# LoRA products on halves of the rows, head sums on quarters of the columns, one partition range for both inverses, and a corrected ordering clock

## The chip, the cores and the metric

One core of a Trainium2 chip. The time is that of the device, from the first to the last instruction of the program, in microseconds (us); several runs are made and their median is compared. The core's engines each work through their own queue, in order: TensorE (PE, with its weight loads shown apart as PEld), VectorE (DVE), ScalarE (ACT), GpSimd (POOL) and SyncE (SP), which here only issues DMAs. PE writes to PSUM, eight banks of 512 float32 in each of 128 partitions. ACT and DVE read the banks.

## The reference

One inference step of a one-layer decoder on 1024 new prompt tokens and 32 sample tokens (8 sequences of 4), with 1024 channels: an RWKV-7 branch and an RG-LRU branch on the same input, gated and merged, an output projection, a layer norm, a SwiGLU feed-forward part and a second layer norm. What matters here is the RWKV-7 branch:

```
w = -softplus(-(w0 + tanh(w_lo) @ w2)) - 0.5        # w_lo: 64 columns of the mixed input
decay = exp(-exp(w))
a = sigmoid(a0 + a_lo @ a2)                         # a_lo: 64 columns
kk = k * k_k;  kk = kk / max(sqrt(sum over the head of kk*kk), 1e-12)
k = k * (1 + (a - 1) * k_a)
per token and head (64 x 64 state S):
    sa = S @ (-kk)
    S  = S * w + outer(sa, kk * a) + outer(v, k)
    y  = S @ r
```

The kernel computes the recurrence in chunks of 64 tokens: inside a chunk a 64 x 64 triangular system per head is inverted (by blocks of 16 and 32), and a state is carried from chunk to chunk. All products that carry weights are done with numbers split in a rounded part (fp32r) and a remainder: three matmuls for one product.

## The kernel before

The tokens are worked in two passes of 512 (in the first with the 32 sample tokens and 8 rows of shift in front, 548 columns in use, in the second 512), the channels in four pairs of 128-channel tiles. A pass and a pair make a **unit** (u, 0 to 7); a unit has two tiles (i), four heads, and for the inverses two halves (g) of four chunks each.

Two kinds of work share PE. The main stream (`gemm_tile`, line of the profile L246 for its matmuls) goes through the input projection tile by tile, 24 wide matmuls for each piece, into two banks in turn; ACT and DVE empty them. Everything else is background: `load2` and `wkv_tile` (LoRA products, decays, rates, head sums), `stage` (copies into the layout of the chunks), `inverse`, `chain` (the recurrence over the eight chunks), `finish`, `lru`, `sample`. Background matmuls use three banks in common (`Bk`) and three of the chain's own. Since a helper records nearly every operation, most instructions have the line L316 in the profile and are told apart by the names of their tiles.

The order on each engine is written out when the kernel is built. Background work is written as generators; between the main stream's matmuls `tick` issues the waiting operations that can start soonest by a **clock** (`Clock`), a table of costs per operation with a time per engine. Where `gemm_tile` or `until` finds nothing free, the clock is advanced. On the chip the engines then run that order, and semaphores make them wait where the clock was wrong.

The places that the change touches:

- `load2(lora, ...)` brings the two LoRA matrices of a unit into `lora`, [128, 2, 2, 128]: w2 (64 rows) on partitions 0 to 63 and a2 on 64 to 127, each in a block of its own with zeros on the other partitions. `wa` holds tanh(w_lo) on partitions 0 to 63 and a_lo on 64 to 127.
- `wkv_tile` multiplies the first block, and then the second, with all 128 rows of `wa` (`bg_mm`, three matmuls a piece; pieces of 292 and 256 columns in the first pass and one of 512 in the second), and ACT takes tanh out of the bank into `t1` and `t4`.
- The head sums: `t6` holds the squares of k; a float32 matmul with `sel` ([128, 128], two columns in use) sums each head's 64 channels. Two rows of the bank go back into `t6` and by four DMAs to a scratch in DRAM (`ssd`), from where `wkv` loads them into `n2` in the layout of the inverses.
- `inverse(u, g)`: a chain of 30 short DVE operations on 64 partitions (`bn`, `bt`, `btmp`), 0 to 63 for g = 0 and 64 to 127 for g = 1; then products with `n2` into `bte` and `bze`, stores to DRAM, loads back (`tdv`, `zt`), and small matmuls on 32 x 32 parts of the array.
- `chain(u)`: for each of eight chunks `cx` (matmuls), a copy of it to `xs`; `cu`, a copy of it to `su`; `cs_`, and four state updates on DVE, (i, h) for a 64-partition half h of tile i:

```
A(xs[0:64, :, 0], cx[0:64])
TC(xs[64:128, :, 1], cx[64:128])
...
A(su[0:64, :, 1, 0], cu[0:64])
TC(su[64:128, :, 1, 1], cu[64:128])
...
for i in range(2):
    for h in range(2):
        STT(to, su[hb, i, 0, h], pc[hb, i, c:c + 1], cs_[hb, i], OP.mult, OP.add)
```

`A` is an ACT activation, `TC` a DVE copy, `STT` a DVE operation of two inputs and a scalar, `MM` a matmul.

Of the kernel before, what the change touches and what calls it, by code (L numbers as in the profile page):

```python
# [9 lines left out]
F32 = mybir.dt.float32  # L10
# [27 lines left out]
C_ID, C_MP, C_SCAN, C_MS, C_MX, C_MB, C_SEL, C_BONES, C_M16, C_N = 0, 128, 256, 768, 832, 896, 904, 1032, 1160, 1161  # L38
# [38 lines left out]
class Clock:  # L77
# [6 lines left out]
    def __init__(self):  # L84
        self.t = dict.fromkeys(("PE", "ACT", "DVE", "POOL", "SP", "DMA"), 0.0)
        self.uses = {}
        self.masks = {}
        self.table = 0
        self.tile = None
        self.port = {"DVE": [], "POOL": []}  # L90
# [86 lines left out]
    def op(self, e, f, args, kw, at, last):  # L177
# [168 lines left out]
def tile_hybrid_step(ctx: ExitStack, tc: tile.TileContext, I, O):  # L346
# [131 lines left out]
    with ExitStack() as zctx:  # L478
# [69 lines left out]
        lora = [T(f"lora{i}", [128, 2, 2, 128], F32R) for i in range(2)]  # L548
# [13 lines left out]
        bn, bt, btmp = T("bn", [128, 16, 16]), T("bt", [128, 16, 16]), T("btmp", [128, 64])  # L562
        bte, bze = T("bte", [128, 16, 32]), T("bze", [128, 16, 32])
        n2s = [T(f"n2_{i}", [128, 16]) for i in range(2)]
# [25 lines left out]
        sel = cst[:, C_SEL:C_SEL + 128]  # L590
# [10 lines left out]
        for x in lora:  # L601
            pool.memset(x.bitcast(F32), 0.0)
# [89 lines left out]
        def load2(dst, src, flag, after):  # L692
# [5 lines left out]
            if len(dst[0].shape) == 3:  # L698
                split2([x.rearrange("p i m -> p (i m)") for x in dst], t[:, 0:256])
            else:  # L700
                for n in range(2):
                    b = slice(64 * n, 64 * n + 64)
                    split2([x[b, n].rearrange("p i m -> p (i m)") for x in dst], t[b, 0:256])
# [4 lines left out]
        def bg_mm(p, ops, use):  # L708

            for t0, t1 in pieces(p):  # L710
# [5 lines left out]
                Bk.put(ps)  # L716
            yield
# [10 lines left out]
        def wkv_tile(u, i, parts, side):  # L728
# [68 lines left out]
        def wkv(u):  # L797
# [14 lines left out]
            for g in range(2):  # L812
                for x in range(2):
                    sp.dma_start(n2[64 * g + 32 * x:64 * g + 32 * x + 32],
                                 ssd[g, :, :, :, 16 * x:16 * x + 16])
# [44 lines left out]
        def inverse(u, g, n2):  # L860
# [3 lines left out]
            pt = slice(64 * g, 64 * g + 64)  # L864
# [34 lines left out]
            for x in range(2):  # L899
                d = slice(16 * x, 16 * x + 16)  # L900
                sp.dma_start(bn[64 * g + 32 * x:64 * g + 32 * x + 32],
# [4 lines left out]
            pool.memset(bt[pt], 0.0)  # L906
            pool.memset(bt[pt].rearrange("p t j -> p (t j)")[:, 0:256:17], 1.0)
# [5 lines left out]
            TT(bn[pt], bn[pt], n2[pt, None, :].to_broadcast([64, 16, 16]), OP.mult)  # L913
            for s in range(15):
                m = 15 - s
                tmp = btmp[pt, 0:m * (s + 1)].rearrange("p (t j) -> p t j", j=s + 1)
                TT(tmp, bn[pt, s, s + 1:16].rearrange("p (t o) -> p t o", o=1).to_broadcast([64, m, s + 1]),
                   bt[pt, s:s + 1, 0:s + 1].to_broadcast([64, m, s + 1]), OP.mult)
                TT(bt[pt, s + 1:16, 0:s + 1], bt[pt, s + 1:16, 0:s + 1], tmp, OP.add)
            for x in range(2):  # L920
                b, d = slice(64 * g + 32 * x, 64 * g + 32 * x + 32), slice(16 * x, 16 * x + 16)
# [4 lines left out]
            for x in range(2):  # L926
                b, d = slice(64 * g + 32 * x, 64 * g + 32 * x + 32), slice(16 * x, 16 * x + 16)
# [59 lines left out]
        def chain(u):  # L987
# [68 lines left out]
            for c in range(8):  # L1056
# [8 lines left out]
                A(xs[0:64, :, 0], cx[0:64])  # L1065
                TC(xs[64:128, :, 1], cx[64:128])
# [10 lines left out]
                A(su[0:64, :, 1, 0], cu[0:64])  # L1077
                TC(su[64:128, :, 1, 1], cu[64:128])
# [11 lines left out]
                for i in range(2):  # L1090
                    for h in range(2):
# [869 lines left out]
```

## Time and profile before

| | |
|---|---|
| median of 3 runs | 2140.77 us (2139.39 to 2144.16) |
| profiled execution, its own time | 2158.58 us |
| its span, first to last instruction | 2156.8 us |
| mean granted clock of PE | 0.962 |
| matmuls, all instructions | 17664, 44027 |
| DMA | 152.85 MB, mean 71 GB/s |

The branches, which hold all that is changed, run to about 1290 us of the span; from 1400 to 2100 us PE does the feed-forward part without a pause.

In a row of the groups stand line, engine, operation, the tiles as out<-in, for PE the rows and columns of the array in use (64*128 is half of the rows), the shape, the count; then busy time, mean length of one, and idle time before. In the timeline stand start and length in us. PE's lengths overlap: how long a matmul holds the array is read from its start to the next one's. float32 matmuls are two instructions each, transposes and the rounded products one.

### The profile page before, as it was taken

The page shows a single profiled execution, that of the slowest core. Times are in us where ns is not written, and L with a number is a line of the kernel's source. Part 1 is how long each engine was busy: PE and PEld are TensorE (multiplying, and loading weights), DVE is VectorE, ACT ScalarE, POOL GpSimd, SP SyncE. Part 2 cuts the span into 40 slices and gives each one's busy share as a digit, 9 for nine tenths or more (in the row PEclk, how much of TensorE's full clock was granted, in tenths as well). Part 3 has the DMA queues.
Part 4 walks back from the last instruction along what each step waited for, and adds up shares of the span by engine and source line. Part 5 has one row for each costly group of instructions (what it writes and reads, how often), then busy time and mean ns, then how long its engine had stood idle before and what let it go on. Part 6 is the DMA issues. An engine that isn't in the chain of part 4 may idle for free.

```text
span 2156.8 us, 44027 instructions
## 1 busy us (share of the span) xinstructions
PE 2065.4 (96%) x17664; PEld 1792.2 (83%) x17664; DVE 1226.6 (57%) x2967; ACT 1070.5 (50%) x2475; POOL 389.2 (18%) x797
## 2 busy tenths in 40 slices
PE   7799999999999999999999899999999999999997
PEld 7788898897986777777777697889999999999987
DVE  5676695796877887777867666522322322222226
ACT  4656756757666677767576735821121122112221
POOL 1101210220310310211212020221211211111124
PEclk9897997999999999999999799999999999999999
DMA  4131231131241231232313323221111211111112
GB/s 137 56 92 36 66 95 48 51 107 51 76 131 60 78 97 52 67 86 67 98 58 90 113 96 133 88 69 38 61 40 35 64 40 47 37 54 49 40 50 81
DMA packets 124925, 152.85 MB, mean 71 GB/s; under 512 B 82784, under 2 KB 87296, under 8 KB 124720
## 3 DMA queue, kind: packets, MB, share of 16 engines
q0 software_dynamic: 31936, 112.75, 15.6%
q1 hardware_dynamic: 92784, 37.28, 7.0%
q8 instruction: 139, 2.28, 0.4%
q14 instruction: 66, 0.54, 0.1%
HBM read 132.45 MB, written 17.57 MB: 70 GB/s over the span
## 4 chain that ended last, share of the span: by engine, by line
PE 76%; DVE 10%; ACT 9%; issue 3%; DMA 1%; POOL 0%; SPq 0%; DVEq 0%; ACTq 0%; POOLq 0%
PE bank L246 60%; PE bank L316 15%; DVE tmp L316 2%; DVE wl L316 1%; ACT tmp L316 1%; ACT wh L316 1%; DVE su L316 1%; ACT L316 1%; ACT arm L316 1%; ACT nz L316 1%; ACT bk L316 1%; DVE btmp L316 1%; DVE bt L316 1%; DVE arm L316 1%; DVE rge L316 1%
## 5 line engine op out<-in xcount | busy, mean ns | idle before, releaser
L246 PE MATMUL bank<-xx,wh 128*128 128x512 f32 (+4 forms) x3168 | 808.3, 342 | 26.9 <-ACT xx L246 8.5
L246 PEld LDWEIGHTS bank<-xx,wh 128*128 128x128 f32 x3168 | 553.5, 196 | 88.7 <-ACT xx L246 8.5
L246 PE MATMUL bank<-xx,wl 128*128 128x512 f32 (+4 forms) x1584 | 541.3, 342 | 0.0
L316 DVE TENSOR_TENSOR wl<-wraw,wh 128x512 fp32r<-128x512 f32 (+2 forms) x336 | 264.3, 788 | 264.2 <-ACT wh L316 262.1
L316 ACT ACTIVATE wh<-wraw 128x512 fp32r<-128x512 f32 (+2 forms) x408 | 246.1, 610 | 274.6 <-PE bank L246 245.6
L246 PE MATMUL bank<-hl,wh 128*128 128x272 f32 (+1 forms) x1056 | 342.6, 324 | 0.9 <-DVE hl L316 0.9
L246 PE MATMUL bank<-hh,wh 128*128 128x272 f32 (+1 forms) x1056 | 341.1, 323 | 0.5 <-ACT hh L316 0.5
L246 PE MATMUL bank<-hh,wl 128*128 128x272 f32 (+1 forms) x1056 | 341.5, 323 | 0.0
L246 PEld LDWEIGHTS bank<-xx,wl 128*128 128x128 f32 x1584 | 310.6, 196 | 28.3 <-issue 3.0
L246 PEld LDWEIGHTS bank<-hh,wh 128*128 128x128 f32 x1056 | 198.7, 188 | 17.3 <-ACT hh L316 1.2
L246 PEld LDWEIGHTS bank<-hl,wh 128*128 128x128 f32 x1056 | 198.7, 188 | 17.2 <-DVE hl L316 1.5
L246 PEld LDWEIGHTS bank<-hh,wl 128*128 128x128 f32 x1056 | 198.6, 188 | 15.3
L316 POOL DMA_DIRECT2D wraw<-in_win x114 | 61.9, 543 | 782.8 <-DVE wl L316 469.1
L316 POOL TENSOR_TENSOR wl<-wraw,wh 128x512 fp32r<-128x512 f32 (+1 forms) x72 | 86.1, 1196 | 513.3 <-ACT wh L316 490.5
L246 PE MATMUL bank<-u,wh 128*128 128x272 f32 (+1 forms) x768 | 176.7, 324 | 0.0
L246 PEld LDWEIGHTS bank<-u,wh 128*128 128x128 f32 x768 | 128.6, 188 | 11.3
L316 DVE TENSOR_TENSOR acc<-acc,bank 128x272 f32<-128x272 f32 (+3 forms) x96 | 49.9, 519 | 148.2 <-PE bank L246 148.2
L316 ACT ACTIVATE sg<-bank 128x272 f32<-128x272 f32 (+1 forms) x66 | 30.8, 466 | 196.1 <-PE bank L246 196.0
L246 PE MATMUL bank<-u,wl 128*128 128x272 f32 (+1 forms) x384 | 124.3, 324 | 0.0
L316 DVE TENSOR_TENSOR sg<-sg,bank 128x272 f32<-128x272 f32 (+1 forms) x66 | 34.3, 520 | 156.1 <-PE bank L246 156.1
L316 ACT ACTIVATE su<-bank 64x256 f32<-64x256 f32 (+1 forms) x192 | 60.2, 337 | 64.6 <-PE bank L316 62.4
L316 ACT ACTIVATE u<-sg 128x272 fp32r<-128x272 f32 (+1 forms) x66 | 33.1, 502 | 112.1 <-DVE sg L316 112.1
(248 smaller groups left out, 3204.2 us busy)
## 6 DMA issues: line engine op xcount, KB each, us to landing
wraw<-in_win POOLq DMA_DIRECT2D x116, 512.0 KB, 3.6
wraw<-in_wgu POOLq DMA_DIRECT2D x48, 512.0 KB, 3.5
wraw<-in_wo POOLq DMA_DIRECT2D x16, 512.0 KB, 3.6
wraw<-in_wdn POOLq DMA_DIRECT2D x16, 384.0 KB, 3.4
wraw<-in_wdn POOLq DMA_DIRECT2D x16, 320.0 KB, 3.2
mgd<-yb POOLq DMA_DIRECT2D x32, 128.0 KB, 2.7
out_y<-tmp SPq DMA_DIRECT2D x8, 512.0 KB
scrN<-nz SPq DMA_DIRECT2D x64, 32.0 KB
```

Source lines behind the costliest of these rows:

```text
L246: fn(*args, **kw)
L316: fn(*args, **kw)
```

## The change

- `lora` becomes [128, 2, 128] without zeros, and is split by one instruction for all 128 partitions. A new function `pair_mm` computes decay and rate together: matmuls of 64 rows, on rows 0 to 63 for the decay and 64 to 127 for the rate, in turn, into two banks at once.
- The head sums of 512 columns become four matmuls of 128 columns with `sel` cut to 32 columns, each into another 32 partitions of one bank (in the first pass one more of 32 columns for the samples); one ACT copy of 128 x 128 takes them out, and four DMAs of another pattern store them.
- `bn`, `bt` and `btmp` are held twice, both on partitions 0 to 63; `bte`, `bze` have 64 partitions and serve both halves; `n2` is [64, 2, 16].
- In `chain` the copies of the lower half go to DVE and those of the upper half to ACT, and the updates run over h outside and i inside.
- The ordering clock: costs for matmuls of few rows or columns are corrected, and ACT and DVE are charged 0.12 us when the first partition of the output changes.

```
 cost(...)
             if args[1].dtype == F32R:
-                return max(0.11, n / 2250)
+                return max(0.11, n / 2250) / (128 // k)
             if k <= 32:
-                return 0.045
+                return 0.045 if n == 32 else 0.024 if k == 32 else 0.017
+            if m < 128 and n > 96:
+                return n / 600 / min(4, 128 // k * (128 // m))
 op(...)
+            if e in ("ACT", "DVE"):
+                part = out.offset // out.ap[0][0]
+                at = max(at, self.t[e] + 0.12 * (self.part.get(e, part) != part))
+                self.part[e] = part
 new function
+        def pair_mm(p, ops, use_a, use_b):
+            for t0, t1 in pieces(p):
+                while len(Bk.free) < 2:
+                    yield
+                pa, pb = Bk.get(), Bk.get()
+                for n, group in enumerate(zip(*ops)):
+                    for ps, (lhsT, rhs, *out) in zip((pa, pb), group):
+                        for w, x, o in ((lhsT, rhs, slice(0, 128)),) if not out else zip(lhsT, rhs, out[0]):
+                            MM(ps[o, :t1 - t0], w, x[:, t0:t1], start=n == 0, stop=n == len(ops[0]) - 1)
+                yield
+                use_a(t0, t1, pa)
+                Bk.put(pa)
+                use_b(t0, t1, pb)
+                Bk.put(pb)
+            yield
 wkv_tile
             t1 = yield from temps.take()
-            yield from bg_mm(p, parts3([x[:, 0, i] for x in lora], wa),
-                             lambda a, b, ps: A(t1[:, a:b], ps[:, :b - a], AF.Tanh, 0.5, D(D_W0H, q)))
+            t4 = yield from temps.take()
+            yield from pair_mm(p, [[(a[s, i], b[s]) for a, b in parts3(lora, wa)] for s in (slice(0, 64), slice(64, 128))],
+                               lambda a, b, ps: A(t1[:, a:b], ps[:, :b - a], AF.Tanh, 0.5, D(D_W0H, q)),
+                               lambda a, b, ps: A(t4[:, a:b], ps[:, :b - a], AF.Tanh, 0.5, D(D_A0H, q)))
             A(t1[:, sl], t1[:, sl], AF.Copy, DECAY_SCALE, DECAY_SCALE)
-            t4 = yield from temps.take()
-            yield from bg_mm(p, parts3([x[:, 1, i] for x in lora], wa),
-                             lambda a, b, ps: A(t4[:, a:b], ps[:, :b - a], AF.Tanh, 0.5, D(D_A0H, q)))
...
-            yield from bg_mm(p, [(sel, t6)], lambda a, b, ps: A(t6[0:2, a:b], ps[0:2, :b - a]))
-            for f in range(2):
-                for g in range(2):
-                    sp.dma_start(ssd[g, i, :, f::2].rearrange("c h t -> h c t"),
-                                 t6[0:2, PO + 256 * g:PO + 256 * g + 256].rearrange("h (c f t) -> f h c t", f=2, t=32)[f])
+            ps = yield from Bk.take()
+            for x in range(4):
+                MM(ps[32 * x:32 * x + 32, 0:128], sel, t6[:, PO + 128 * x:PO + 128 * x + 128], start=True, stop=True)
+            if p == 0:
+                MM(ps[0:32, 128:160], sel, t6[:, SO:ZO], start=True, stop=True)
+            yield
+            A(t6[:, PO:PO + 128], ps[:, 0:128])
+            if p == 0:
+                A(t6[0:32, SO:ZO], ps[0:32, 128:160])
+            Bk.put(ps)
+            for x in range(4):
+                g, c = x // 2, 2 * (x % 2)
+                sp.dma_start(ssd[g, i, c:c + 2].rearrange("c (h f) t -> h c (f t)", h=2),
+                             t6[32 * x:32 * x + 2, PO:PO + 128].rearrange("h (c m) -> h c m", c=2))
 inverse
-            pt = slice(64 * g, 64 * g + 64)
+            bn, bt, btmp, n2 = bns[g], bts[g], btmps[g], n2[:, g]
...
-                b, d = slice(64 * g + 32 * x, 64 * g + 32 * x + 32), slice(16 * x, 16 * x + 16)
+                b, d = slice(32 * x, 32 * x + 32), slice(16 * x, 16 * x + 16)
 chain
-                A(xs[0:64, :, 0], cx[0:64])
-                TC(xs[64:128, :, 1], cx[64:128])
+                TC(xs[0:64, :, 0], cx[0:64])
+                A(xs[64:128, :, 1], cx[64:128])
...
-                A(su[0:64, :, 1, 0], cu[0:64])
-                TC(su[64:128, :, 1, 1], cu[64:128])
+                TC(su[0:64, :, 1, 0], cu[0:64])
+                A(su[64:128, :, 1, 1], cu[64:128])
...
-                for i in range(2):
-                    for h in range(2):
+                for h in range(2):
+                    for i in range(2):
```

More of the change, by code (lines that the diff above doesn't have):

```diff
@@ L35 @@
 (D_W0H, D_A0H, D_KKH, D_NKK, D_KAH, D_KAQ, D_BAH, D_BIH, D_SP4, D_NSP4) = range(10)
-C_ID, C_MP, C_SCAN, C_MS, C_MX, C_MB, C_SEL, C_BONES, C_M16, C_N = 0, 128, 256, 768, 832, 896, 904, 1032, 1160, 1161
+C_ID, C_MP, C_SCAN, C_MS, C_MX, C_MB, C_SEL, C_BONES, C_M16, C_N = 0, 128, 256, 768, 832, 896, 904, 936, 1064, 1065
 SPLITS = [(0, 5), (5, 5), (10, 6), (16, 6)]
@@ L89, in __init__ @@
         self.tile = None
+        self.part = {}
         self.port = {"DVE": [], "POOL": []}
@@ L547, in tile_hybrid_step @@
         sg = [T(f"sg{i}", [128, W], F32R) for i in range(2)]
-        lora = [T(f"lora{i}", [128, 2, 2, 128], F32R) for i in range(2)]
+        lora = [T(f"lora{i}", [128, 2, 128], F32R) for i in range(2)]
         g2 = [T(f"g2{i}", [128, 2, 128], F32R) for i in range(2)]
@@ L561, in tile_hybrid_step @@
         p1 = T("p1", [128, 8, 32])
-        bn, bt, btmp = T("bn", [128, 16, 16]), T("bt", [128, 16, 16]), T("btmp", [128, 64])
-        bte, bze = T("bte", [128, 16, 32]), T("bze", [128, 16, 32])
-        n2s = [T(f"n2_{i}", [128, 16]) for i in range(2)]
+        bns, bts, btmps = [[T(f"{n}{g}", [64, *d]) for g in range(2)]
+                           for n, d in (("bn", (16, 16)), ("bt", (16, 16)), ("btmp", (64,)))]
+        bte, bze = T("bte", [64, 16, 32]), T("bze", [64, 16, 32])
+        n2s = [T(f"n2_{i}", [64, 2, 16]) for i in range(2)]
         n2x = [T(f"n2x{i}", [4, 32]) for i in range(2)]
@@ L589, in tile_hybrid_step @@
         maskB = cst[:, C_MB:C_MB + 8]
-        sel = cst[:, C_SEL:C_SEL + 128]
+        sel = cst[:, C_SEL:C_SEL + 32]
         bones = cst[:, C_BONES:C_BONES + 128]
@@ L600, in tile_hybrid_step @@
             pool.memset(x, 0.0)
-        for x in lora:
-            pool.memset(x.bitcast(F32), 0.0)
         sp.dma_start(h0s, I["h0"])
@@ L697, in load2 @@
             sp.dma_start(t[:, 0:256], src)
[L698 to L703, printed above, removed]
+            split2([x.rearrange("p i m -> p (i m)") for x in dst], t[:, 0:256])
             temps.put(t)
@@ L813, in wkv @@
                 for x in range(2):
-                    sp.dma_start(n2[64 * g + 32 * x:64 * g + 32 * x + 32],
+                    sp.dma_start(n2[32 * x:32 * x + 32, g],
                                  ssd[g, :, :, :, 16 * x:16 * x + 16])
@@ L900, in inverse @@
                 d = slice(16 * x, 16 * x + 16)
-                sp.dma_start(bn[64 * g + 32 * x:64 * g + 32 * x + 32],
+                sp.dma_start(bn[32 * x:32 * x + 32],
                              scrN[g][:, :, d, d].rearrange("c x s t -> (c x) s t"))
@@ L905, in inverse @@
                 yield
-            pool.memset(bt[pt], 0.0)
-            pool.memset(bt[pt].rearrange("p t j -> p (t j)")[:, 0:256:17], 1.0)
+            pool.memset(bt, 0.0)
+            pool.memset(bt.rearrange("p t j -> p (t j)")[:, 0:256:17], 1.0)
             for i in range(2):
@@ L912, in inverse @@
                 yield
-            TT(bn[pt], bn[pt], n2[pt, None, :].to_broadcast([64, 16, 16]), OP.mult)
+            TT(bn, bn, n2[:, None, :].to_broadcast([64, 16, 16]), OP.mult)
             for s in range(15):
                 m = 15 - s
[L916 to L919, printed above, removed]
+                tmp = btmp[:, 0:m * (s + 1)].rearrange("p (t j) -> p t j", j=s + 1)
+                TT(tmp, bn[:, s, s + 1:16].rearrange("p (t o) -> p t o", o=1).to_broadcast([64, m, s + 1]),
+                   bt[:, s:s + 1, 0:s + 1].to_broadcast([64, m, s + 1]), OP.mult)
+                TT(bt[:, s + 1:16, 0:s + 1], bt[:, s + 1:16, 0:s + 1], tmp, OP.add)
             for x in range(2):
-                b, d = slice(64 * g + 32 * x, 64 * g + 32 * x + 32), slice(16 * x, 16 * x + 16)
+                b, d = slice(32 * x, 32 * x + 32), slice(16 * x, 16 * x + 16)
                 TT(bte[b, :, d], bt[b], n2[b, None, :].to_broadcast([32, 16, 16]), OP.mult)
@@ L926, in inverse @@
             for x in range(2):
-                b, d = slice(64 * g + 32 * x, 64 * g + 32 * x + 32), slice(16 * x, 16 * x + 16)
+                b, d = slice(32 * x, 32 * x + 32), slice(16 * x, 16 * x + 16)
                 TT(bze[b, :, d], bt[b].rearrange("p t j -> p j t"),
```

## The prediction

> **What bounds the kernel now.** I read the page first: the busy row and the shares of the chain of waits. Lines from which nothing follows are left out.
>
> ```profile
> PE 2065.4 (96%) x17664; PEld 1792.2 (83%) x17664; DVE 1226.6 (57%) x2967; ACT 1070.5 (50%) x2475; POOL 389.2 (18%) x797
> ...
> PE 76%; DVE 10%; ACT 9%; issue 3%; DMA 1%; POOL 0%; SPq 0%; DVEq 0%; ACTq 0%; POOLq 0%
> ```
>
> TensorE (PE) is the bound: 96% busy and 76% of the chain. VectorE (DVE) and ScalarE (ACT) hold 10% and 9% of it, which is 216 and 194 us of the 2156.8 us span, so 18 of every 100 us that either of them works lie on the path. Next the busy times by stretch: every line that the change touches runs between about 43 and 1290 us.
>
> ```profile
> 300.00:400.00 100.00, 95.84 (x1189) 82.73 (x1189) 61.87 (x192) 63.58 (x162) 12.22 (x42) 0.83 0.19 55
> ...
> 700.00:800.00 100.00, 98.15 (x591) 75.10 (x592) 82.91 (x196) 69.17 (x150) 27.15 (x72) 1.00 0.27 84
> ...
> 100.00:1300.00 1200.00, 1151.63 (x11982) 964.17 (x11981) 887.24 (x2324) 788.62 (x1866) 206.95 (x577) 0.95 0.27 78
> ```
>
> The columns are busy time and instructions of PE, weight loads, DVE, ACT and POOL, then the granted clock. In the long stretch PE is idle 48.4 us in 1200 and the clock is 0.95; DVE is busy 74%, ACT 66%. So a microsecond of PE work that goes here should nearly be a microsecond of time. Last, who PE waits for between 100 and 1290 us, the two longest entries:
>
> ```profile
> PE bank L316 <- DVE zt L316: 15.0, 6, 3.7
> PE bank L316 <- DVE su L316: 8.1, 13, 1.5
> ```
>
> Of the 48.4 us, 23.1 are waits on DVE in the inverses (zt) and the chain of states (su): DVE was later than the order written out expected.
>
> **The change part by part. First the decay and rate products.** 144 matmuls become 144 of half the rows, laid alternately on rows 0 to 63 and 64 to 127. The first row is the view by tile, the others are the timeline of PE (start, length, count).
>
> ```profile
> L316 PE MATMUL bank<-wa,lora x144: 274/301/794, 43.2 to 1100.5; 128*128 128x292 f32 x48, 128*128 128x256 f32 x48, 128*128 128x512 f32 x48
> ```
>
> ```profile
> 43.18 0.57 PE L316 MATMUL bank<-wa,lora 128*128 128x292 f32 x3
> 43.59 0.43 PE L246 MATMUL bank<-xx,wh 128*128 128x300 f32 x2
> ...
> 278.14 0.71 PE L316 MATMUL bank<-arm,bk 64*128 64x128 f32 x4
> 278.78 0.50 PE L246 MATMUL bank<-xx,wh 128*128 128x256 f32 x2
> ...
> 906.70 0.40 PE L246 MATMUL bank<-xx,wl 128*128 128x512 f32 x1
> 906.93 0.40 PE L246 MATMUL bank<-xx,wh 128*128 128x512 f32 x1
> 907.25 1.26 PE L316 MATMUL bank<-arm,bk 64*128 64x128 f32 x16
> 908.45 0.50 PE L246 MATMUL bank<-xx,wh 128*128 128x512 f32 x1
> 908.78 0.40 PE L246 MATMUL bank<-xx,wl 128*128 128x512 f32 x1
> ```
>
> Lengths overlap, so costs are read from start to start. Three matmuls of 292 columns take 0.41 (0.137 each; by columns 0.120 for 256), one of 512 takes 0.23. A tile of the first half of the sequence costs 3 x 2 x (0.137 + 0.120) = 1.54 us, one of the second half 6 x 0.23 = 1.38.
>
> Do halves of the rows run side by side? The 16 matmuls at 907.25 use both halves with 128 columns each, 0.107 apiece (a quarter of the 0.43 found below for 512). One by one they would need 1.71 us; they took 1.20, ideal pairs 0.86. So they do, for plain float32; for the rounded type (fp32r) of these products no row shows it. I take it that they do, since the halves are the same.
>
> What does it cost to go from the whole array to a part and back? 906.93 to 907.25 is 0.32 where 0.23 is normal (0.09 to go in); the four on one half at 278.14 need 0.43 and take 0.64 (0.21 more); the second wide matmul after it comes 0.33 after the first (0.10 more). A round trip costs 0.40 us, and every piece of these products makes one: 16 pieces in the first half, 8 in the second.
>
> After: second half 0.69 + 0.40 = 1.09, saving 0.29 x 8 = 2.3 us. First half 0.77 + 2 x 0.40 = 1.57, losing 0.03 x 8 = 0.2. Sum **-2.1 us**. Bounds: not side by side, +0.40 x 24 = +9.6; every piece beside other work in the same shape, so that no trip is paid, -(0.77 + 0.69) x 8 = -11.7.
>
> The Trainium skill, page TensorEngine Tiling (Array Packing), section Overview, gives up to 2x for a contraction of 64 or less and up to 4x for 32 output columns, and its section Tiling Modes adds that a change of mode drains the array without saying for how long. By the speedups alone this term would be -11.7 us and the next one -10.6 (three quarters of 14.2, below).
>
> The pair also takes two of the three background banks at once, where one after the other would do. What waits is a background task, and the wide products go on meanwhile: nothing. With no cover it is at most a copy out of a bank (0.58 us, the row of ACT below) for each of the 24 pieces, +14.
>
> **Head sums by quarters of the columns.**
>
> ```profile
> L316 PE MATMUL bank<-tmp,cst x48: 378/483/697, 56.2 to 1107.4; 128*128 128x292 f32 x16, 128*128 128x256 f32 x16, 128*128 128x512 f32 x16
> ```
>
> ```profile
> 1061.92 1.02 PE L316 MATMUL bank<-tmp,cst 128*128 128x512 f32 x2
> 1062.37 0.80 PE L246 MATMUL bank<-xx,wl 128*128 128x512 f32 x1
> 1063.01 0.39 PE L246 MATMUL bank<-xx,wh 128*128 128x512 f32 x1
> ...
> 1084.23 0.39 PE L246 MATMUL bank<-xx,wl 128*128 128x512 f32 x1
> 1084.55 0.46 PE L316 MATMUL bank<-su,bkt 128*64 128x64 f32 x8
> 1084.93 0.24 PE L316 MATMUL bank<-zt,p 32*32 32x16 f32 x6
> ```
>
> From 1061.92 to 1063.01 is 1.09, less one wide matmul of 0.23: 0.86 us for two instructions, 0.43 each. The first half (548 columns) costs 0.92. Together 8 x 0.86 + 8 x 0.92 = 14.2 us. After: eight instructions of 128 columns, two on each quarter. The nearest row is the group at 1084.55: eight of 64 columns, four on each half of the columns, at best 4 x 0.053 = 0.21, the same as 2 x 0.107 here; it took 0.38 to the next start. With 0.09 to go in and 0.10 behind: 0.57 us, in the first half 0.62 (two more of 32 columns). Saved 0.29 x 8 + 0.30 x 8 = **-4.7 us**. Bounds: one quarter after the other, 0.64 more each, +5.5; no trips, -(0.65 + 0.66) x 8 = -10.5.
>
> Around it, one copy of 128x128 by ACT takes the place of one or two of two rows (row below); four stores per tile stay four on SP's queue, with the same loads behind them.
>
> ```profile
> L316 ACT ACTIVATE tmp<-bank 2x512 f32<-2x512 f32 x8 | 4.7, 583 | 7.1 <-PE bank L316 6.9
> ```
>
> **Copies swapped, state updates by half, inverses on partitions 0 to 63.** Timelines of DVE and ACT:
>
> ```profile
> 515.13 1.16 DVE L316 SCALAR_TENSOR_TENSOR su<-su,pc,bank 64x64 f32<-64x64 f32 x4 [0.83 <-PE bank L316]
> ...
> 519.79 0.29 DVE L316 COPY xs<-bank 64x128 f32<-64x128 f32 x1
> 520.11 0.69 DVE L316 TENSOR_TENSOR tmp<-tmp,pcs 128x512 f32<-128x512 f32 x1
> 520.72 0.72 DVE L316 TENSOR_TENSOR tmp<-tmp 128x548 f32<-128x548 f32 x1
> ```
>
> ```profile
> 519.41 0.27 ACT L316 ACTIVATE xs<-bank 64x128 f32<-64x128 f32 x1 [1.17 <-PE bank L316]
> 519.58 0.68 ACT L316 ACTIVATE bkh<-bk,pc 128x128 f32<-128x128 f32 x2
> ```
>
> 520.72 starts 0.08 before its predecessor ends, both from partition 0; 520.11 starts 0.03 after the copy that wrote partitions 64 to 127. On ACT, 519.58 starts 0.10 early behind a copy to partition 0. So a change of first partition costs DVE about 0.095 and ACT about 0.11.
>
> Per step of the chain (64 steps) DVE's two copies move to partition 0: up to four changes fewer, 0.38 us. The four updates run 0, 0, 64, 64 instead of 0, 64, 0, 64: two fewer, 0.19, and these lie in the step's own latency (1.16 becomes 0.97). That is 24 + 12 = 36 us of DVE. In the eight second inverses, 30 short instructions each, every foreign instruction between them cost two changes: between 0 and 30 x 0.19 x 8 = 46 us; no row counts them, and I take a quarter, 11. DVE sheds 47 us, 18% of it on the path: **-8.5 us**. ACT takes the upper copies: up to four more changes a step, 0.11 x 4 x 64 = 28 us, less some 5 for the head sums' 16 copies (0.58 to the 0.27 of 519.41): +23, 18% of it: **+4.1 us**. The ends are all and nothing on the path: -47 and +28. The LoRA weights' split in one instruction instead of two, the smaller constants and the two memsets that go weigh under 3 us of ACT and DVE and are put at nothing; PE's backlog hides them. bte and bze are now shared by both inverses, so a write waits for the other's store to have read; the 30 instructions of an inverse stand between them, which hide it.
>
> **The ordering clock.** It only changes the order in which the work is issued. It now charges changes of partition, so PE should find su and zt late less often. Between all of the 23.1 us gained and as much lost I take half of su's 8.1: **-4 us**.
>
> **Sum**: -2.1 - 4.7 - 8.5 + 4.1 - 4 = -15.2, call it -15. Against the profiled execution's 2158.6 us (1.8 around its span) that is 2143.6; the median of the runs is 2140.8, 17.8 below that execution, and the forecast is **2126 us**.
>
> **The rivals.**
>
> *The order does the most.* No trip paid in most places, and PE's waits for DVE gone: -11.7 - 10.5 - 4.4 - 23 is the end, -50; with half of the trips saved and half of the waits, -14.5 - 4.4 - 11.5 = -30: 2110 us. For it: 48.4 us of PE idle to be had. Against it: the ticker takes the earliest task, not the one in the shape that the array is in.
>
> *The halves of the fp32r products do not run side by side.* +9.6 - 4.7 - 8.5 + 4.1 - 4 = -3.5: 2137 us. Against it: the 907.25 row; for it: that row is another type.
>
> *Off the path.* The chain of states, not PE, sets the length between 100 and 1290 us, and the PE work saved turns into idle: 2140 us. Against it, idle of 4%.
>
> *ACT behind DVE, which ends slower.* The two copies of a step read one bank and run one after the other, ACT first, as the wait shows:
>
> ```profile
> DVE su L316 <- ACT su L316: 66.4, 39, 5.0
> ```
>
> After, ACT waits for DVE, and DVE is the busier one. Behind ACT's copy stand evacuations for which PE's wide products need their two banks back. If each of the 128 copies is 0.8 us later and three tenths of that reaches PE, it costs 31 us: with the -15, 2156 us. It decides from 15 us, 0.12 us of PE per copy. Against it: DVE has 47 us less to do.
>
> *The clock.* 300 to 400 us, with 1189 matmuls, was granted 0.83; 700 to 800, with 591, 1.00. If the new order crowds the small ones, 0.02 of clock over 1200 us costs 25 us: 2151 us, deciding from 0.012. Against it: there are only 96 more matmuls (the head sums'), beside 11982. The Trainium skill, TensorE: Matmul & The Clock Gate, Part 1, says that a monitor of PE's activity halves the clock after an idle window; it puts the cause in idleness, which the trace's 95.84 us busy at 0.83 neither shows nor excludes, as overlapping lengths count as busy.
>
> **How the numbers follow.** Forecast 0.50; the order does the most 0.16; not side by side 0.11; off the path 0.10; ACT behind DVE 0.08; the clock 0.05. A measurement of this kernel can tell about 0.2% (4.3 us) from no change. Faster is the first two and half of the third, 0.72; slower the last two and a little of off the path, 0.15; the rest, 0.13, is the same. The forecast's own range is 2115 to 2136; 8 in 10 reaches most of the second case and of the slow ones' near side: 2104 to 2147.
>
> **What would show it.** The products as rows of 64*128 with three pairs of 512 columns in about 0.7 us, 0.09 ahead and 0.1 to 0.2 behind; the head sums as 128*32, eight in about 0.4. Four updates in 0.97 instead of 1.16. PE's idle time between 100 and 1300 us at 48 or less, and the wait of DVE su for ACT su turned round. I am wrong if PE's matmuls shrink and its idle time grows by as much, if the clock there falls below 0.94, or if ACT's waits for DVE exceed the 66 us that stood the other way.

## The result, and the profile after

The changed kernel takes **2159.12 us** (median of 4 runs, 2154.14 to 2159.69) against 2141.66 us of the kernel before on the same chip (4 runs, 2139.39 to 2144.16): ratio 1.0068, 95% interval [1.0043, 1.0093]. By the ratio it is 15 us slower (the medians are 17 us apart) where 15 us faster were forecast; the range ended at 2147. The kernel before was measured again beside each experiment, and there its medians were 2145.6 to 2149.1 us. Against these the loss is 10 to 14 us.

The profiled execution of the changed kernel took 2154.14 us (span 2152.4, clock 0.970), less than the 2158.58 us of the one before (clock 0.962). The two executions are not typical of their kernels: the profile of before lies 17 us above its median, that of the changed kernel is the fastest of its four runs. So these two spans aren't compared, only what stands in the rows. First the busy row and the shares of the chain of waits, then the stretch from 100 to 1300 us:

```profile
PE 2059.0 (96%) x17760; PEld 1771.5 (82%) x17760; DVE 1187.1 (55%) x2959; ACT 1076.9 (50%) x2468; POOL 390.0 (18%) x795
...
PE 82%; ACT 9%; DVE 7%; issue 2%; DMA 1%; POOL 0%; DVEq 0%; ACTq 0%; POOLq 0%
```

```profile
100.00:1300.00 1200.00, 1145.63 (x12076) 944.63 (x12075) 851.18 (x2322) 800.50 (x1867) 207.92 (x577) 0.96 0.26 79
```

PE has 6 us less work and DVE 40 us less, much as forecast (47); ACT has 6 us more, where 23 were forecast. But PE's idle time in the stretch did not fall: 54.4 us where it was 48.4. (One kernel profiled twice, h1 and h1b below, had 51.4 and 55.0, so the rise is not much more than two executions differ by.) Who PE waits for there:

```profile
PE bank L255 <- DVE rge L325: 16.0, 3, 6.6
...
PE bank L325 <- DVE su L325: 4.7, 5, 2.1
...
PE bank L325 <- ACT su L325: 4.5, 6, 1.3
...
PE bank L325 <- ACT bkh L325: 4.2, 6, 1.4
...
PE bank L325 <- DVE zt L325: 0.2, 1, 0.2
```

The wait on the inverses (zt) went from 15.0 to 0.2 us and that on su from 8.1 to 4.7, as the new clock should make it. In their place stand 16.0 us in three waits of the main stream itself (`rge`: the bank of the input projection that DVE empties) and waits on ACT (`su` 2.2 before, `bkh` 1.7). And the two engines of the copies wait for each other:

```profile
DVE su L325 <- PE bank L325: 81.9, 58, 3.6
DVE wl L325 <- ACT wh L325: 76.3, 74, 3.9
...
ACT xs L325 <- DVE xs L325: 63.4, 41, 4.7
ACT su L325 <- DVE su L325: 52.6, 45, 2.4
```

The same rows before:

```profile
DVE wl L316 <- ACT wh L316: 42.6, 49, 3.6
...
DVE su L316 <- PE bank L316: 35.9, 28, 3.4
DVE xs L316 <- ACT xs L316: 35.5, 30, 2.7
```

ACT now waits 116.0 us for DVE's two copies. Before, it was DVE that waited (66.4 + 35.5 = 101.9 us). DVE also waits longer for ACT in the splitting of the weights (`wl`, 42.6 to 76.3). The prediction had named as a sign of its being wrong that ACT's waits for DVE exceed 66 us. That figure is `su` alone, which now stands at 52.6; only both copies together exceed it. The waits turned round as expected and grew a little. What is new beside them is the longer wait the other way, in `wl`.

### The profile page after: what moved, and what is told of

Read it like the earlier page. It is cut to its first block, busy times and chain, and to the rows that moved or that the text cites. A ratio compares the mean times of both kernels' runs of the same rounds, so it can differ in the third digit from the quotient of the medians.

```text
span 2152.4 us, 44131 instructions
## 1 busy us (share of the span) xinstructions
PE 2059.0 (96%) x17760; PEld 1771.5 (82%) x17760; DVE 1187.1 (55%) x2959; ACT 1076.9 (50%) x2468; POOL 390.0 (18%) x795
## 4 chain that ended last, share of the span: by engine, by line
PE 82%; ACT 9%; DVE 7%; issue 2%; DMA 1%; POOL 0%; DVEq 0%; ACTq 0%; POOLq 0%
PE bank L255 66%; PE bank L325 16%; DVE tmp L325 2%; ACT tmp L325 1%; ACT wh L325 1%; ACT arm L325 1%; DVE wl L325 1%; ACT L325 1%; ACT bk L325 1%; ACT accB L325 1%; ACT nz L325 0%; DVE su L325 0%; ACT su L325 0%; DVE yb L325 0%; DVE rge L325 0%
## 5 line engine op out<-in xcount | busy, mean ns | idle before, releaser
L255 PEld LDWEIGHTS bank<-xx,wh 128*128 128x128 f32 x3168 | 546.2, 194 | 105.3 <-ACT tmp L325 13.3
L255 PEld LDWEIGHTS bank<-xx,wl 128*128 128x128 f32 x1584 | 306.1, 193 | 30.1 <-issue 4.1
L325 ACT ACTIVATE su<-bank 64x256 f32<-64x256 f32 (+1 forms) x192 | 65.7, 342 | 61.4 <-DVE su L325 52.6
```

The lines of the kernel that those rows point to most:

```text
L255: fn(*args, **kw)
L325: fn(*args, **kw)
```

## The experiments

Two theories stood at the start, beside a third that came up with the trace. **Copies**: with DVE's copy first, ACT is held behind the busier engine, and that is the loss. **Order**: the corrected clock plans a worse order. **Trips**: the pieces of the products and sums cost more, in changes between the whole array and its parts, than they save; the order splits a piece's group of six in 13 of 24 pieces.

The order is planned when the kernel is built, so that any edit plans another one. To keep it, each choice of the planner was recorded for one kernel and played back for another ("in the order of"): every engine then issues the same sequence, but for the edit named. Ratios are to the kernel before, measured beside on the same chip. Between two ratios the difference is given, its half-width as the root of the sum of the squares of theirs.

**The new clock alone, and the change with the old clock.**

```
e2: kernel before + the new lines of cost(...) and op(...)
e1: changed kernel - the new lines of cost(...) and op(...)
```

> The kernel before with the new clock alone (all three of its edits), nothing else changed. Theory Order (the new clock writes out an order that is worse on the chip in the second pass, from about 600 us on, where the profile of the change lost 33 us): slower than before, 2150 to 2165 us. Theory Copies (ACT's copies behind DVE's are what costs) and theory Trips (the going in and out of parts of the array costs): the same as before or faster, 2130 to 2145.

> All of the change but the clock, which is that of before. Theory Order: the products, sums and places give what the prediction said without the order, 2126 to 2138 us. Theory Copies and theory Trips: it stays slow, 2150 to 2165.

Measured: the new clock alone 2140.96 us, **0.9977** [0.9957, 0.9997]; the change with the old clock 2154.64, **1.0060** [1.0035, 1.0084]. The ordering clock is not the loss; Order falls in this form. With the new clock alone the waits on the inverses go and the waits on `rge` come, as in the changed kernel:

```profile
PE bank L255 <- DVE rge L325: 11.8, 4, 5.6
...
PE bank L255 <- ACT rge L325: 7.0, 2, 3.6
...
PE bank L325 <- DVE zt L325: 0.7, 1, 0.7
```

**Copies and updates in the old order, and the old places in the new order.**

```
h2: kernel before, in its own order
-                A(xs[0:64, :, 0], cx[0:64])
-                TC(xs[64:128, :, 1], cx[64:128])
+                TC(xs[0:64, :, 0], cx[0:64])
+                A(xs[64:128, :, 1], cx[64:128])
                 (su likewise; updates: h outside, i inside)
a1: changed kernel, in its own order: the same lines put back, and bn, bt,
    btmp, bte, bze, n2 of g = 1 again on partitions 64 to 127
```

> The kernel before with its own order of issue kept operation for operation (the list of picks is recorded and played back); only the two copies of a chain step change engines (lower half to DVE, upper half to ACT) and the four updates run with the half outside. PE, POOL and SP have the same instructions in the same order. The prediction's step (36 us of DVE shed, 28 us more on ACT, 18% of either on the path): about 1.5 us faster, so the same within 5 us. Theory Copies: 8 to 20 us slower than before.

> The changed kernel with its own order of issue kept operation for operation; copies, updates and the inverses' partitions are put back to where they were before, and the products by halves, the sums by quarters stay. By the prediction's step the changed places are worth 4.4 us, so 2163 us. Theory Order: 2157 to 2168, no better than the change. Theory Copies: 2140 to 2150, most of the loss is gone.

Measured: swap and updates in the old order 2170.06 us, **1.0118** [1.0090, 1.0147], 25 us, more than the 8 to 20 that Copies expected and slower than the whole change. The old places in the new order 2153.29, **1.0025** [1.0005, 1.0046]: better than the changed kernel, not as good as the one before. That lies between the ranges of Copies (2140 to 2150) and Order (2157 to 2168) and confirms neither; it puts back three things at once.

**Updates alone, swap alone.**

```
h1: h2 without the swap        h3: h2 without the updates
```

> The kernel before with every engine's order of issue kept instruction for instruction, except that the four state updates of a step run half by half (0, 0, 64, 64) instead of 0, 64, 0, 64. The prediction's step (two changes of first partition fewer per step, 0.19 us in the step's own latency, 64 steps): 0 to 5 us faster than the kernel before, the group of four in 0.97 instead of 1.16 us. Copies (ACT's copies held behind DVE's are the loss): the swap is not in here, so no loss; 2136 to 2147 as well. If this kernel is slower by 5 us or more, the updates are part of the loss and both theories are short.

> The kernel before with every engine's order kept, except that in each step DVE copies the lower halves of xs and su and ACT the upper ones. Copies: all of the loss of the earlier kernel with swap and updates (1.0118 times the kernel before) is here: 1.008 to 1.016, ACT waiting over 100 us for DVE's two copies. The prediction's step (DVE sheds 24 us, ACT takes 28, 18% of each on the path): within 3 us of the kernel before, ratio 0.998 to 1.002.

Measured: updates 2140.13 us, **0.9964** [0.9942, 0.9986]; swap 2176.17, **1.0125** [1.0103, 1.0147], 27 us. The whole loss of h2 is in the swap, and the updates gain.

**The swap with ACT reading first.** Both copies of a step read one bank, and the framework lets the second reader wait for the first. To tell the order of the readers from the change of partitions, the step was mirrored:

```
h4: h3 with
-                TC(xs[0:64, :, 0], cx[0:64])
-                A(xs[64:128, :, 1], cx[64:128])
+                A(xs[64:128, :, 1], cx[64:128])
+                TC(xs[0:64, :, 0], cx[0:64])
-                for h in range(2):          (matmuls of cu and cs_)
+                for h in (1, 0):            (su likewise)
e6: changed kernel with the same edit, planned anew by its own clock
```

> The kernel before with every engine's order kept, and the step mirrored: DVE copies the lower halves and ACT the upper ones as in the changed kernel, but ACT's copy is issued first and so reads the bank first, and the matmuls that use the copies take the upper half first. Against the kernel before only the partitions change hands; against the kernel with the copies swapped (1.0125 times the kernel before) only the order of the two readers. Copies (ACT held behind DVE's copy is the whole price): the loss goes, 0.997 to 1.002. If the price is in the partitions (ACT's upper half, its changes of first partition): 1.008 to 1.015 again. The prediction's step (DVE sheds 24 us, ACT takes 28, 18% on the path): 0.998 to 1.001, so that it can't be told from Copies.

> The changed kernel, planned by its own clock, with the step mirrored: halves as in the changed kernel, ACT's copy issued first, the matmuls that use the copies upper half first. Copies: about the changed kernel with the copies put back (1.0006 times the kernel before), 0.997 to 1.003; if DVE's fewer changes of partition are worth what the prediction gave them, 4 us under that. If the price is in the partitions: 1.006 as the changed kernel.

Measured: in the old order 2153.59 us, **1.0023** [1.0001, 1.0045], just above the range of Copies (to 1.002) and far from that of the partitions (1.008 to 1.015). So the order of the two readers is worth 0.0102 ± 0.0031, 22 us, of the swap's 27. (The matmuls that read the copies are turned with it, so that in both kernels the first copy feeds the first of them.) In the changed kernel 2141.25 us, **0.9980** [0.9957, 1.0002], which is 0.0088 ± 0.0033 or 19 us under the changed kernel, but in an order planned anew. The partitions by themselves cost at most a little (0.0023 ± 0.0022).

The timelines of the two engines show how. With DVE reading first, in the order of the kernel before (start, length, [idle before <- for whom]); DVE, then ACT:

```profile
663.09 0.27 DVE L323 COPY xs<-bank 64x128 f32<-64x128 f32 x1
664.64 0.69 DVE L323 TENSOR_TENSOR wl<-wraw,wh 128x512 fp32r<-128x512 f32 x1 [1.29 <-ACT wh L323]
...
668.81 0.28 DVE L323 COPY su<-bank 64x128 f32<-64x128 f32 x1
```

```profile
663.39 0.27 ACT L323 ACTIVATE xs<-bank 64x128 f32<-64x128 f32 x1 [1.28 <-DVE xs L323]
663.69 0.40 ACT L323 ACTIVATE bkh<-bk,pc 128x128 f32<-128x128 f32 x1
664.00 0.61 ACT L323 ACTIVATE wh<-wraw 128x512 fp32r<-128x512 f32 x1
...
669.12 1.06 ACT L323 ACTIVATE su<-bank 64x128 f32<-64x128 f32 x3 [1.63 <-DVE su L323]
```

ACT stands 1.28 us for DVE's copy. The weights' first half `wh` is behind that copy on ACT, so it is late. DVE's `wl`, which needs it, then waits 1.29 us for ACT. Behind `wl` on DVE stand six more operations and the next copy, and for that copy ACT waits 1.63 us. The waits go round. Here is the same step of the same order with ACT first (the mirrored step); it comes 9 us earlier in the span. DVE, then ACT:

```profile
654.16 0.28 DVE L323 COPY xs<-bank 64x128 f32<-64x128 f32 x1
654.56 0.69 DVE L323 TENSOR_TENSOR wl<-wraw,wh 128x512 fp32r<-128x512 f32 x1
...
658.75 0.28 DVE L323 COPY su<-bank 64x128 f32<-64x128 f32 x1
```

```profile
653.30 0.27 ACT L323 ACTIVATE xs<-bank 64x128 f32<-64x128 f32 x1
...
653.91 0.62 ACT L323 ACTIVATE wh<-wraw 128x512 fp32r<-128x512 f32 x1
...
657.52 1.07 ACT L323 ACTIVATE su<-bank 64x128 f32<-64x128 f32 x3
```

ACT copies without waiting for DVE, `wh` is ready when DVE comes to `wl`, and DVE's copy to `su` follows its copy to `xs` after 4.59 us, where it took 5.72. In other steps DVE waits for ACT's copy; no row of the view of waits has ACT waiting for DVE's.

The Trainium skill (PSUM — Partial Sum Buffer, section PSUM bank collisions raise a hardware error) wants two engines kept apart by bank and group of 32 partitions, and says that different groups of one bank may be accessed at the same time. The two copies read different groups, so by that rule neither would have to wait; the program makes the second wait all the same. No run here took that wait away, so what it would bring stays open.

Over the long stretch, DVE first (the swap alone):

```profile
DVE su L323 <- PE bank L323: 99.5, 66, 5.7
...
DVE wl L323 <- ACT wh L323: 69.7, 67, 3.6
...
ACT xs L323 <- DVE xs L323: 68.1, 46, 3.9
...
ACT su L323 <- DVE su L323: 56.7, 45, 4.0
...
PE bank L323 <- ACT su L323: 8.8, 14, 1.4
...
PE bank L323 <- ACT tmp L323: 6.0, 8, 1.9
```

ACT first (mirrored):

```profile
DVE su L323 <- ACT su L323: 67.3, 40, 5.3
...
DVE wl L323 <- ACT wh L323: 47.7, 56, 2.5
...
DVE xs L323 <- ACT xs L323: 40.0, 35, 3.1
...
PE bank L323 <- ACT tmp L323: 3.1, 5, 1.2
...
PE bank L323 <- ACT su L323: 0.3, 1, 0.3
```

PE's waits for ACT's `su` and `tmp` are 14.8 us with DVE first and 3.4 with ACT first; all its waits for ACT in the stretch are 26.9 and 14.6. The chain itself is longer too: from the first to the last of ACT's eight copies `xs` of a unit, summed over the eight units, 518.3 us against 493.5. The two profiles are 24.3 us apart in span (2172.4 and 2148.1). PE's idle time (span less busy time) is 11.6 of that, 105.8 and 94.2; the rest stands in its busy time (2066.6 and 2053.9), with a granted clock of 0.966 and 0.969. How much of the rest is the clock was not separated.

**The changed kernel with the copies put back.** Once planned anew, and once in the changed kernel's own order:

```
e4: changed kernel, copies as before      a2: e4 in the changed kernel's order
```

> The changed kernel, planned by its own clock, with the two copies of a step put back (ACT the lower half, DVE the upper); all the rest of the change stays. Copies: the loss goes; at or under the kernel before, 2125 to 2145, and 12 us or more under the changed kernel. Trips (the pieces of the products and sums cost more in changes of the array's mode than they save, since the order splits their groups): 2145 to 2155. The prediction's steps without DVE's copies would give 2128.

> The changed kernel with its own order kept instruction for instruction, and only the two copies of a step put back (ACT the lower half, DVE the upper, ACT first). Copies: the changed kernel (1.0068 times the kernel before) less the 0.9% to 1.25% that the swap cost in the other orders: 0.994 to 0.999. Beside the kernel with the old updates and inverse partitions as well (1.0025) it gives what these two are worth in this order: 0.2 to 0.4% by the updates' 0.36%, so 0.998 to 1.001. If it stays at 1.004 or more, the swap is not the loss in the changed kernel's own order.

Measured: planned anew 2150.71 us, **1.0006** [0.9983, 1.0030]; in the own order 2146.37, **0.9979** [0.9954, 1.0003]. Planned anew it is above the time that Copies gave (2125 to 2145) and within that of Trips (2145 to 2155), which the next two runs test by themselves. In its own order it is where Copies expected it: the swap costs the changed kernel 0.0089 ± 0.0035, 19 us by the ratios, though the medians are only 13 us apart (beside a2 the kernel before took 2148.7 us, beside the changed kernel 2141.7). The granted clocks differ too, 0.970 to 0.973 in a2's ten runs and 0.966 to 0.970 in the changed kernel's four. At 0.970, which both reached, stand 2154.14 us for the changed kernel and 2148.89 to 2149.85 for a2, and the chain from first to last `xs`, summed as above, is 547.0 and 538.8. So in this order the loss by the swap is there, but its size isn't settled, and whether it is the whole loss isn't either. The rest of the change is worth 0.2%, some 4 us, not 15. Beside a1 (the old updates and inverse partitions as well, 1.0025) these two parts gain 0.0046 ± 0.0032.

**Products and sums on the whole array.**

```
a3: a1 with
-  (a[s, i], b[s])   for s in (rows 0 to 63, rows 64 to 127)
+  (a[:, n, i], b)   for n in range(2)      (zeros in the other rows)
a4: a1 with
-  MM(ps[32 * x:32 * x + 32, 0:128], sel, ..., start=True, stop=True)
+  MM(ps[:, 0:128], sel[:, 96 - 32 * x:224 - 32 * x], ..., start=x == 0, stop=x == 3)
```

> The kernel with the changed kernel's order and the old copies, updates and inverse partitions (measured at 1.0025 times the kernel before), with the two products of each piece taken again over all 128 rows (zeros in the other half of the weights), one after the other in the same two banks and at the same places of the order, so that no piece changes the array's mode. The prediction's step (24 pieces, each a round trip of 0.40 us, saving 2.1 us in all): 2 us slower than that kernel. Trips (what the split groups cost is more than the rows save): 5 us or more faster than it, at or under the kernel before.

> The kernel with the changed kernel's order and the old copies, updates and inverse partitions (1.0025 times the kernel before), with its head sums taken on the whole array: four matmuls of 128 columns that accumulate in one bank, each with its two columns of weights at rows 0, 32, 64 or 96, at the same places of the order; the copy out and the stores stay. The prediction's step: the four on the quarters take 0.57 us with the trip in and out, the four on the whole array 0.43, less some for the wider columns, so 2 us faster to 5 us slower (by its sum of 4.7 saved, 4.7 slower). Trips: 3 us or more faster than that kernel.

Measured: products on all rows 2155.07 us, **1.0033** [1.0017, 1.0049], so the halves gain 0.0008 ± 0.0026; sums on the whole array 2159.39, **1.0053** [1.0028, 1.0078], so the quarters gain 0.0028 ± 0.0032, 6 us. Trips expected both at least 3 us faster than a1, and neither is; Trips falls. Neither gain can be told from nothing by itself.

**Clock and updates together, planned anew.**

> The kernel before with the new clock alone (0.9977 times the kernel before) and the four updates half by half (0.9964 in the old order), planned anew: without copies, products, sums and inverses of the change. Copies and the sum of the single edits: 0.992 to 0.998, the fastest so far and under both kernels. If the order planned anew is worth as much as the edits, either way: 0.996 to 1.003.

Measured: 2159.19 us, **1.0048** [1.0020, 1.0075]. Two edits that gain 0.23% and 0.36% by themselves lose 0.5% together, once the order is planned anew. That is outside both ranges that were expected (up to 0.998, and up to 1.003). It pointed to the planning.

**One constant of the clock nudged, nothing else.**

```
n1: kernel before       -    LOOK = 0.5       +    LOOK = 0.52
n2: kernel before       -    "POOL": 0.13     +    "POOL": 0.135
n3: e6                  -    LOOK = 0.5       +    LOOK = 0.52
```

> The kernel before, with one constant of the ordering's clock nudged (how far ahead of TensorE a task may start, 0.50 to 0.52 us): the same instructions in another order. If the order planned anew moves the time by itself: off by 0.3% or more to either side. If the order only matters where a rule of it changes: 0.998 to 1.002.

> The kernel before, with another constant of the ordering's clock nudged (the fixed cost of a GpSimd instruction, 0.130 to 0.135 us). If the order planned anew moves the time by itself: off by 0.3% or more to either side, and not by the same as the other nudge. If not: 0.998 to 1.002.

> The changed kernel with ACT's copy first (0.998 times the kernel before), and the same nudge (0.50 to 0.52 us). If the order planned anew moves the time by itself: 0.992 to 1.004 and not at 0.998; if not: 0.996 to 1.000.

Measured: n1 2173.95 us, **1.0105** [1.0071, 1.0139]; n2 2167.32, **1.0075** [1.0049, 1.0102]; n3 2156.35, **1.0023** [1.0001, 1.0045], 0.0043 above the kernel it nudges. The same instructions in another order, from a constant moved by 4%, are 16 to 23 us slower. Part of n1's loss goes with the granted clock: all its six runs were granted 0.959 to 0.962, and the 27 runs of the kernel before beside them 0.963 to 0.974. n2's clock (0.967 to 0.973) does not differ. In n1 PE is idle 60.0 us of the stretch instead of 48.4:

```profile
100.00:1300.00 1200.00, 1139.99 (x11862) 948.87 (x11861) 880.18 (x2312) 789.09 (x1866) 206.19 (x572) 0.94 0.27 77
```

**Two parts of the change with no new order.** The updates, and the sums by quarters at the old sums' places:

```
b1: kernel before, in its own order, + updates by h + four sums of 128 columns
h1b: h1 once more, on the same chip
```

> The kernel before with every engine's order kept, the four updates half by half, and the head sums by quarters of the columns (four matmuls of 128 columns where one or two of 512 or 548 stood; the sample's 32 columns at the second piece's place; the copies out and the four stores at their old places). If the parts gain and only the order anew loses: the updates' 0.36% and the sums' 0.28%, 0.991 to 0.996, under the kernel before and the changed kernel. By the prediction's terms: 4.7 us for the sums and up to 5 for the updates. If the sums lose by their trips in this order: 0.997 to 1.001.

> The kernel before with only the updates half by half, once more (0.9964 with an interval of 0.9942 to 0.9986 before): 0.994 to 0.999. Beside it on the same chip the sums of the other kernel show by themselves: 3 to 8 us between the two if they gain.

Measured: b1 2140.97 us, **0.9979** [0.9963, 0.9996], not the 0.991 to 0.996 that the two gains added up to; h1b 2143.30, **0.9983** [0.9963, 1.0003]. The updates' two measurements give 0.9974 ± 0.0015 together, 6 us. The sums add nothing that can be seen here (0.0004 ± 0.0026). b1, the updates alone (h1) and the new clock alone (e2) are all about 0.2% under the kernel before and well under the changed one; which of them is the fastest can't be told.

## Why the prediction was wrong, point by point

**The step that failed is the price of the swapped copies: "DVE sheds 47 us, 18% of it on the path", -8.5 us, against +4.1 us for what ACT takes over.** It priced the swap by the work that each engine gains and loses. That work was put somewhat high: mirrored, the swap moves DVE's busy time from 1226.6 to 1215.1 us (11.5, where up to 24 were counted) and ACT's from 1070.5 to 1090.8 (20.3 of 28). The mirrored kernel costs 0.2%, which the step's own +0.7 us for the copies (24 us at 18% off, 28 on) does not contradict. (DVE's price for a change of first partition, 0.095 us, is not what the rows shown there give, 0.08 + 0.03 = 0.11. The difference is worth under 2 us of the sum.) What the step left out is that the swap also turns round which engine reads the bank first. In the old order that costs 22 us (h3 against h4), in the changed kernel by the ratios 19. The second figure is less sure: a2 puts the partitions back as well and shows 13 us by the medians, and e6 has an order of its own.

The prediction had this as the rival **ACT behind DVE**, at 2156 us, with 0.8 us later per copy, three tenths of it reaching PE, and deciding from 0.12 us of PE per copy. 19 to 22 us are 0.15 to 0.17 us for each of the 128 copies: past that point, at about two thirds of the rival's 31 us. Its route was another. It had the wide products wait for their banks, but their waits for ACT in the stretch are 2.6 us before and 2.9 with the swap alone; what rose is those of the background's matmuls (8.2 to 24.0). What spoke against the rival ("DVE has 47 us less to do") did not decide it. `wl` already makes DVE wait for ACT, and a wait the other way closes a circle, as the step at 663 us shows.

**Decay and rate products, -2.1 us:** right in its mechanism. Halves of fp32r do run side by side, for which no row of before stood (timeline of PE, changed kernel):

```profile
42.85 0.67 PE L325 MATMUL bank<-wa,lora 64*128 64x292 f32 x6
43.45 0.54 PE L255 MATMUL bank<-xx,wh 128*128 128x300 f32 x2
...
960.59 0.96 PE L325 MATMUL bank<-wa,lora 64*128 64x512 f32 x6
961.48 0.50 PE L255 MATMUL bank<-xx,wl 128*128 128x512 f32 x1
961.82 0.63 PE L255 MATMUL bank<-xx,wh 128*128 128x512 f32 x2
...
1047.03 0.49 PE L325 MATMUL bank<-wa,lora 64*128 64x512 f32 x1
1047.45 0.73 PE L255 MATMUL bank<-xx,wh 128*128 128x512 f32 x2
```

Six of 292 columns take 0.60 us to the next start, where two groups of three took 0.82. Six of 512 take 0.89, and the first wide matmul behind them 0.34 instead of 0.23: 1.00 us, 1.09 in the prediction, 1.38 before. Not foreseen was that the order splits the groups. In 11 of 24 pieces the six stand together; in most of the others one stands alone, as at 1047.03, where it takes 0.42 us for its 0.23. The term came out at 0.0008 ± 0.0026 (a3 against a1): 2 us, with an uncertainty of 6. The bound of +9.6 for halves one after the other is excluded by the rows. The Trainium skill (TensorEngine Tiling (Array Packing), Tiling Modes) has the change of mode drain the array, and the 0.42 us of the lone matmul agrees; by the page's speedups alone the term would have been -11.7, which the runs don't show.

**Head sums, -4.7 us:** in the changed kernel's order 6 us (a4 against a1), which agrees but can't be told from nothing. The group itself is as expected:

```profile
1059.05 0.40 PE L255 MATMUL bank<-xx,wh 128*128 128x512 f32 x1
1059.37 0.42 PE L325 MATMUL bank<-tmp,cst 128*32 128x128 f32 x8
1059.73 0.50 PE L255 MATMUL bank<-xx,wh 128*128 128x512 f32 x1
1060.07 0.39 PE L255 MATMUL bank<-xx,wl 128*128 128x512 f32 x1
```

From 1059.05 to 1060.07 there are two wide matmuls (0.46) and the sums: 0.56 us, 0.57 in the prediction, 0.86 before. In the old order the gain was not to be seen (b1 against h1b), and both figures have uncertainties of 6 to 7 us.

**Updates by half:** the group of four takes 0.96 us, 0.97 in the prediction, 1.16 before.

```profile
522.82 0.96 DVE L325 SCALAR_TENSOR_TENSOR su<-su,pc,bank 64x64 f32<-64x64 f32 x4
```

Their 12 us of DVE were put at 18%, 2.2 us; they gave 6 ± 3 (0.9974). They lie in the step's own latency, as the prediction said itself, so a share taken over all of DVE may be too low for them. **Inverses on one range of partitions** were only measured with the updates in the changed kernel's order, 10 us for both with an uncertainty of 7; by themselves they were not tried.

**The ordering clock, -4 us:** the clock alone gave 5 ± 4 us (e2), but not by the step's reason alone. The waits on `su` and `zt` went, as expected, and the waits on `rge` came, which the prediction did not have: 12 to 16 us for DVE (1.5 before), so most of what was gained is given back there. More than that, the term was treated as a property of the clock. A new order of this kernel can move the time by more than the terms: +16 and +23 us for two nudges of the kernel before, +9 for one on the changed kernel with ACT first. So what the rest of the change (a2, -4 us) lacks to the forecast's -15 is within what planning anew does. That this is its cause is not shown, since the whole change was never played in the old order, and stays open.

**The other rivals.** "The halves do not run side by side" is refuted by the rows above. "The clock": 0.96 in the stretch of the profile, not under 0.94; over whole runs 0.966 to 0.970, where the kernel before had 0.961 to 0.976 beside the experiments. "Off the path" doesn't describe it: the swap makes it slower, not the same.

## What to carry to other kernels

When two engines read one bank one after the other, it can matter which of them reads first. Here ACT first was the better, which DVE already follows elsewhere. Look at the waits between the two engines in both directions before moving work from one to the other, since a wait turned round can close a circle that no share of busy time shows. Where an order is planned by a clock and the kernel before holds one order of many, measure what a nudge of the planner does first: here that was 16 to 23 us for two nudges, more than any gain under study. An edit is then judged in a fixed order, and the new order by itself.

## What the runs showed of the hardware

The scatter between runs of one kernel is mostly the granted clock: of a1's ten runs the fastest took 2145.06 us at a mean clock of 0.974, and the slowest 2159.23 at 0.967. That is about 2 us for 0.001 of clock. The profile of before was one at 0.962, that of the changed kernel one at 0.970; by this estimate the 0.008 is worth 16 us, enough to make the span of the faster kernel the longer one. Small gains need the same care: the updates alone (h1) had a mean clock of 0.972 where the kernel before beside them had 0.968, 8 us by the same estimate, as much as their gain in that run. In h1b the clocks were 0.970 and 0.969.

The granted clock is not only chance. The nudged order n1 had a lower one in each of its runs than the kernel before in any run beside it, so the order of the same instructions seems to move the clock too. By the estimate the difference of the means, 0.961 and 0.968, is some 15 of n1's 23 us.

Four float32 matmuls on four quarters of the columns overlap: eight instructions of 128 columns take 0.36 us to the next start (1059.37 above), where one by one at 0.107 they would take 0.86.
